# Three first-product blocks kept in SBUF across the end of the gate-table stage

## The chip, the core and the metric

The kernel runs on one core of a Trainium2 chip. The metric is the device time of one execution in microseconds; times of before are the median of three runs and one profiled execution. Engines are named as in the profile: PE is TensorE, PEld its weight load, DVE is VectorE, ACT is ScalarE, POOL is GpSimd, SP is SyncE, whose only work is to issue DMAs.

## The reference, cut to what matters

Two layers, each a token mixer and then an expert channel mixer ("PEER") over 16384 experts. The change touches the channel mixer alone:

```python
def peer(h, wq, keys, u_tab, v_tab):
    q = (t @ wq).reshape(T, PEER_HEADS, 2, PEER_DHALF)
    s = jnp.einsum('thpd,hpkd->thpk', q, keys)
    sv, si = lax.top_k(s, PEER_TOPK)
    ...
    experts = jnp.take_along_axis(cidx, fi, axis=-1)
    gates = jax.nn.softmax(fv, axis=-1)
    ...
        a = jax.nn.gelu(jnp.einsum('tkd,td->tk', u_tab[ec], xc))
        return jnp.einsum('tk,tkd->td', a * gc, v_tab[ec])
```

Each token picks 128 experts (8 heads, 16 each), takes the gelu of its product with their rows of `u_tab`, weights it with the gates, and sums their rows of `v_tab`.

## The kernel before

For most tokens the kernel does not gather: it computes all 16384 experts densely and multiplies by a gate table that is zero where an expert was not picked. The experts come in 128 blocks of 128. For block i, `u_phase(i)` loads a 512 KB weight tile (`u_t`), splits it into two parts (`load_split`: ScalarE makes `whi`, VectorE `wlo`), makes the first product with 24 matmuls (`proj`, L314 to L316) and lets ScalarE take the gelu into an SBUF tile `a` (L824). Such a block is called a projection block. Later `prep` multiplies `a` by the block's gates (L1047, VectorE) and splits the result into `ahi` (L1052, ScalarE) and `alo` (L1053, VectorE), and the second product with rows of `v_tab` follows, again 24 matmuls per 512 KB tile (L1089 to L1091 in layer 0, L1073 in layer 1): a value block.

A layer's channel mixer has three stages:

1. The top-k search (`topk`), on VectorE for the most part.
2. The gate table: for each 16 tokens VectorE makes four one-hot products (`oj`, `oi`, two `wo`; L981 to L986), TensorE multiplies them (L994), ScalarE brings the result to SBUF (`gs`, L996), stores 1 MB to the DRAM table `gd` (L998) and copies the first eight blocks' part to `gt` (L999), which group 0 of the loop uses. There are 32 such steps in layer 0 and 24 in layer 1.
3. The expert loop: 16 groups of 8 blocks. Each group loads its gates (`gt` from `gd`, L1033), preps its 8 blocks and runs its value blocks; in layer 0 the results are added to `x_l` by VectorE (L1092), in layer 1 they stay in PSUM.

While stages 1 and 2 run, TensorE computes projection blocks ahead of the loop: `AHEAD` = 70 of the 128 in layer 0 and 62 in layer 1, spread evenly over the block numbers. Since they do not fit, ScalarE stores each to the DRAM buffer `ad` (L826) and `prep` reads it back (L1043). `upto`, called after each step of the two stages, says how many blocks and how many gather jobs should have been issued by then, from `AHP`, `AHT`, `TKP` and `TKT`. The other 58 (66) blocks are computed in the loop, in `prep`.

For the tokens that are not treated densely (256 in layer 0, 128 in layer 1) GpSimd gathers one row per partition (L835) and VectorE takes a dot (`u_job`, L840) or adds a weighted row (`v_job`, L851): 512 and 256 jobs, each with a 512 KB gather. In the loop `pace` spreads what is left of them over the steps.

The order on each engine is not that of the code: the framework's scheduler sets it when the program is built. Buffers come from pools. A pool that is opened where another was closed takes its bytes, and its first tiles wait for the last users of the old ones. Before, the pools of stage 2 are opened in the order `gsp` (two table tiles `gs` of 8 KB per partition), `mid` (the picks), `spill` (two `a` tiles), then working tiles; after them, at the same place, the loop opens four `ahi`/`alo` pairs (layer 0), `stash` (five `a` tiles), `rx` (three more buffers for `raw` tiles) and six more pairs. `raw` tiles, weights and gathers alike, take turns in a ring of six buffers plus, in the loop, these three.

## Time and profile before

| | us |
|---|---|
| median of 3 runs | 3904.5 (3897.5 to 3907.6) |
| profiled execution | 3904.18 |
| its span, first to last instruction | 3902.4 |
| TensorE busy | 3644.7 (93%), weight loads 3038.8 (78%) |
| VectorE busy | 3208.8 (82%) |
| ScalarE busy | 1493.1 (38%) |
| GpSimd busy | 1064.6 (27%) |

In the profiled execution layer 0's gate table runs from about 973 to 1221 and its expert loop to about 2326; layer 1's gate table ends at about 3063, its loop at 3902. A row of a timeline gives start, duration, engine, line, operation and tiles, and in brackets how long the engine sat idle before it and what ended that. DMA records give the issue, not the landing: when a transfer has landed is read from who waited for it. The engines' busy share is a mean over stages with different limits, so the stages are read apart.

### The profile page before, as it was taken

Reading aid. Unit: us, or ns where it says so; the run is one execution under the profiler, and the core shown is the slowest. Engines: PE = TensorE matmul, PEld = TensorE weight load, DVE = VectorE, ACT = ScalarE, POOL = GpSimd, SP = SyncE. Lnnn points to the kernel's source line nnn. Section 1 sums busy time; section 2 is a strip of 40 time slices with the busy share of each in tenths; the row PEclk is TensorE's granted clock in tenths of the full one; section 3 lists DMA queues with packets and bytes.
Section 4 is the critical chain, followed back from the end, with each engine's and each line's share of the span. In section 5 each row is a group of like instructions: output and inputs, shape, how many; then the busy total and the mean of one; then the engine's idle time right before and its main releaser. Section 6 shows DMA issues by size and latency. Waiting matters only on the chain.

```text
span 3902.4 us, 52533 instructions
## 1 busy us (share of the span) xinstructions
PE 3644.7 (93%) x18725; PEld 3038.8 (78%) x18725; DVE 3208.8 (82%) x6734; ACT 1493.1 (38%) x2115; POOL 1064.6 (27%) x782
## 2 busy tenths in 40 slices
PE   8989889999996999999999989898999999999998
PEld 4777777877775777777777777678999888888887
DVE  7865799998998888888988878548999788788887
ACT  4244433323665222222322233433348533333333
POOL 0000001144332454445555510000000334344441
PEclk9989889999997999999999999899999999999999
DMA  7711134488997999899999947004457999999995
GB/s 249 224 48 45 43 97 157 152 299 289 338 348 277 320 332 313 320 318 335 332 329 323 339 173 251 22 1 141 130 174 285 321 344 341 343 348 337 345 343 187
DMA packets 377663, 967.04 MB, mean 248 GB/s; under 512 B 30632, under 2 KB 160472, under 8 KB 369848
## 3 DMA queue, kind: packets, MB, share of 16 engines
q1 hardware_dynamic: 239048, 468.13, 35.4%
q0 software_dynamic: 111280, 406.28, 29.3%
q10 hardware_dynamic: 27072, 89.27, 5.8%
q8 instruction: 147, 2.41, 0.2%
q14 instruction: 116, 0.95, 0.1%
HBM read 872.20 MB, written 91.36 MB: 247 GB/s over the span
## 4 chain that ended last, share of the span: by engine, by line
PE 41%; issue 10%; DMA 7%; DVE 6%; POOL 5%; ACT 2%; ACTq 0%; POOLq 0%; SPq 0%; DVEq 0%
PE sc L1073 9%; PE mm L314 6%; PE mm L315 6%; PE mm L316 6%; POOL raw L835 5%; PE tp L1073 4%; DMA raw<-in_v_n_dram,E 2%; PE sc L1089 2%; PE sc L1090 2%; PE sc L1091 2%; DVE ht L851 1%; DMA gt<-gd 1%; DVE wlo L163 1%; PE mm L592 1%; DMA raw<-in_u_n_dram,E 1%
## 5 line engine op out<-in xcount | busy, mean ns | idle before, releaser
L162 ACT ACTIVATE whi<-raw 128x1024 fp32r<-128x1024 f32 x640 | 676.5, 1060 | 1501.0 <-PE mm L315 612.3
L835 POOL DMA_INDIRECT raw<-in_u_n_dram,E x384 | 511.2, 1331 | 2226.2 <-DVE wlo L163 1031.4
L314 PE MATMUL mm<-hi_l,whi 128*128 128x512 f32 (+1 forms) x2656 | 995.9, 375 | 11.8 <-ACT whi L162 5.7
L316 PE MATMUL mm<-hi_l,wlo 128*128 128x512 f32 (+1 forms) x2656 | 988.9, 372 | 7.6 <-DVE wlo L163 7.5
L315 PE MATMUL mm<-lo_l,whi 128*128 128x512 f32 (+1 forms) x2656 | 990.7, 373 | 4.5 <-DVE lo_l L294 4.3
L163 DVE TENSOR_TENSOR wlo<-raw,whi 128x1024 fp32r<-128x1024 f32 x640 | 781.2, 1223 | 178.4 <-ACT whi L162 169.9
L835 POOL DMA_INDIRECT raw<-in_v_n_dram,E x384 | 547.7, 1426 | 545.8 <-DVE ht L851 268.6
L314 PEld LDWEIGHTS mm<-hi_l,whi 128*128 128x128 f32 x2656 | 502.7, 189 | 85.5 <-ACT whi L162 6.4
L316 PEld LDWEIGHTS mm<-hi_l,wlo 128*128 128x128 f32 x2656 | 502.2, 189 | 78.0 <-DVE wlo L163 13.5
L315 PEld LDWEIGHTS mm<-lo_l,whi 128*128 128x128 f32 x2656 | 502.9, 189 | 76.9 <-DVE lo_l L294 9.3
L840 DVE SCALAR_TENSOR_TENSOR raw<-raw,ht 128x1024 f32<-128x1024 f32 x384 | 465.9, 1223 | 102.3 <-DMA raw<-in_u_n_dram,E 101.6
L851 DVE SCALAR_TENSOR_TENSOR ht<-raw,wg,ht 128x1024 f32<-128x1024 f32 x381 | 488.6, 1283 | 41.3 <-DMA raw<-in_v_n_dram,E 38.9
L1089 PE MATMUL sc<-ahi,whi 128*128 128x512 f32 x1024 | 399.7, 398 | 34.2 <-DVE x_l L1092 30.5
L1090 PE MATMUL sc<-alo,whi 128*128 128x512 f32 x1024 | 407.4, 399 | 24.4 <-DVE alo L1053 23.6
L1091 PE MATMUL sc<-ahi,wlo 128*128 128x512 f32 x1024 | 404.1, 395 | 0.9 <-DVE wlo L163 0.9
L1052 ACT ACTIVATE ahi<-a 128x512 fp32r<-128x512 f32 (+1 forms) x256 | 147.0, 577 | 394.2 <-DVE a L1047 392.6
L1089 PEld LDWEIGHTS sc<-ahi,whi 128*128 128x128 f32 x1024 | 194.3, 190 | 87.1 <-DVE x_l L1092 23.5
L1090 PEld LDWEIGHTS sc<-alo,whi 128*128 128x128 f32 x1024 | 195.5, 191 | 77.5 <-DVE alo L1053 38.4
L996 ACT ACTIVATE gs<-sc 128x1024 f32<-128x1024 f32 x112 | 214.1, 2021 | 64.0 <-PE sc L994 59.6
L1091 PEld LDWEIGHTS sc<-ahi,wlo 128*128 128x128 f32 x1024 | 195.6, 191 | 41.7 <-DVE wlo L163 1.8
L1047 DVE TENSOR_TENSOR a<-a,gt 128x512 f32<-128x512 f32 (+1 forms) x256 | 158.0, 621 | 64.6 <-DMA gt<-gd 39.7
L1053 DVE TENSOR_TENSOR alo<-a,ahi 128x512 fp32r<-128x512 f32 (+1 forms) x256 | 157.5, 622 | 11.7 <-ACT ahi L1052 11.3
(310 smaller groups left out, 4933.5 us busy)
## 6 DMA issues: line engine op xcount, KB each, us to landing
raw<-in_u_t_dram SPq DMA_DIRECT2D x256, 512.0 KB
raw<-in_v_b_dram SPq DMA_DIRECT2D x128, 512.0 KB
raw<-in_v_n_dram SPq DMA_DIRECT2D x128, 512.0 KB
gd<-gs ACTq DMA_DIRECT2D x56, 1024.0 KB
raw<-in_w_adt_dram SPq DMA_DIRECT2D x64, 512.0 KB
gt<-gd SPq DMA_DIRECT2D x15, 2048.0 KB
raw<-in_wq_dram SPq DMA_DIRECT2D x48, 512.0 KB
gt<-gd SPq DMA_DIRECT2D x15, 1536.0 KB
```

The lines of the kernel that those rows point to most:

```text
L162: nc.scalar.activation(hi, raw, AF.Copy)
L163: nc.vector.tensor_tensor(lo, raw, hi.bitcast(F32), op=ALU.subtract)
L314: nc.tensor.matmul(ps, whi[:, k], hhi[:, k], start=(k == 0), stop=False)
L315: nc.tensor.matmul(ps, whi[:, k], hlo[:, k], start=False, stop=False)
L316: nc.tensor.matmul(ps, wlo[:, k], hhi[:, k], start=False, stop=(k == K - 1))
L835: nc.gpsimd.indirect_dma_start(out=g, out_offset=None, in_=tab, in_offset=bass.IndirectOffsetOnAxis(ap=G["E"][:, it, k:k + 1], axis=0), el ...
L840: nc.vector.scalar_tensor_tensor(g, g, 1.0, G["ht", it], op0=ALU.mult, op1=ALU.mult, accum_out=G["dots", it][:, k:k + 1])
L851: nc.vector.scalar_tensor_tensor(G["acc", it], g, G["wg", it][:, k:k + 1], G["acc", it], op0=ALU.mult, op1=ALU.add)
L1073: nc.tensor.matmul(accs[t][h], w[:, sl], v[:, halves[h]], start=(i == 0 and j == 0), stop=(i == NKEYS - 1 and j == 2))
L1089: nc.tensor.matmul(ps, vh[:, c], wh, start=(c == 0), stop=False)
L1090: nc.tensor.matmul(ps, vh[:, c], wl, start=False, stop=False)
L1091: nc.tensor.matmul(ps, vl[:, c], wh, start=False, stop=(c == GS - 1))
```

## The change

Three more blocks per layer are computed ahead, at the end of the gate-table stage: the first three block numbers that are not spilled (0, 2 and 4 in layer 0; 0, 1 and 3 in layer 1). They are not stored; `upto` keeps the tile in `kept`, and `prep` takes it from there. `AHT` grows by three, so that the schedule of blocks ends at 73 and 65. In the loop these blocks no longer call `u_phase` nor `pace`, and the number of steps over which jobs are spread is smaller by six. For the tiles to survive, the pool `stash` is opened before the gate-table stage, at the other end of SBUF, and serves that stage's spilled blocks too; `spill` lives only in the top-k stage; and `gsp` is opened within the gate-table stage, behind `mid`.

```diff
-AHT = [50, 38]
+AHT = [53, 41]
...
+CARRY = 3
...
             spilled = sorted(order)
+            carry = [i for i in range(NKEYS) if i not in order][:CARRY]
+            early = spilled + carry
+            kept = {}
...
             def upto(nu, nt):
-                while nxt[0] < min(nu, AHEAD[l]):
-                    u_phase(spilled[nxt[0]])
+                while nxt[0] < min(nu, len(early)):
+                    kept[early[nxt[0]]] = u_phase(early[nxt[0]])
                     nxt[0] += 1
                 tick(nt - done[0])
...
             with ExitStack() as es1:
-                gsp = es1.enter_context(tc.tile_pool(name=nm("gsp"), bufs=2))
                 mid = es1.enter_context(tc.tile_pool(name=nm("mid"), bufs=1))
-                cur["st"] = es1.enter_context(tc.tile_pool(name=nm("spill"), bufs=SPB))
...
                 with ExitStack() as es2:
+                    cur["st"] = es2.enter_context(tc.tile_pool(name=nm("spill"), bufs=SPB))
                     tp_ = es2.enter_context(tc.tile_pool(name=nm("topk"), bufs=1))
...
+                cur["st"] = es.enter_context(tc.tile_pool(name=nm("stash"), bufs=STB, side="right"))
                 with ExitStack() as es2:
+                    gsp = es2.enter_context(tc.tile_pool(name=nm("gsp"), bufs=2))
                     tw = es2.enter_context(tc.tile_pool(name=nm("gw"), bufs=2))
...
             with ExitStack() as es2:
                 vps = [] if last else [es2.enter_context(tc.tile_pool(name=nm("vp"), bufs=4))]
-                cur["st"] = es2.enter_context(tc.tile_pool(name=nm("stash"), bufs=STB))
...
-                nstep = (NKEYS - AHEAD[l]) * PWU[l] + NKEYS - PEND[l]
+                nstep = (NKEYS - AHEAD[l] - CARRY) * PWU[l] + NKEYS - PEND[l]
...
                         nc.sync.dma_start(A, ad[order[i], :, :TD])
+                    elif i in carry:
+                        A = kept.pop(i)
                     else:
                         A = u_phase(i)
...
-                    if i not in order:
+                    if i not in order and i not in carry:
                         pace(PWU[l])
```

What the scheduler made of it is seen in the order of instructions. The program up to the end of layer 0's top-k search is the same. In all three places below a row is line, operation, output tile and input tiles; line numbers of the changed kernel are one to six higher.

ScalarE, end of layer 0's gate table and the first preps of group 0. `gs` and `gt` are the last table tile and its copy, `whi` splits of weights, `a` a gelu. Before:

```order
L998 DMA gd<-gs_11470 128x2048
L999 ACTIVATE gt_5781<-gs_11470 128x128
L1052 ACTIVATE ahi_11670<-a_11667 128x512
L1052 ACTIVATE ahi_11686<-a_11683 128x512
L162 ACTIVATE whi_11746<-raw_11744 128x1024
L162 ACTIVATE whi_11803<-raw_11801 128x1024
L1052 ACTIVATE ahi_11724<-a_11721 128x512
L1052 ACTIVATE ahi_11740<-a_11737 128x512
L843 ACTIVATE wg_121<-dots_120 128x128
L162 ACTIVATE whi_11857<-raw_11855 128x1024
L162 ACTIVATE whi_11895<-raw_11893 128x1024
L824 ACTIVATE a_11775<-mm_11750 128x512
```

And now:

```order
L1003 DMA gd<-gs_11576 128x2048
L1004 ACTIVATE gt_5781<-gs_11576 128x128
L1058 ACTIVATE ahi_11736<-a_11646 128x512
L1058 ACTIVATE ahi_11743<-a_11740 128x512
L1058 ACTIVATE ahi_11748<-a_11679 128x512
L1058 ACTIVATE ahi_11755<-a_11752 128x512
L1058 ACTIVATE ahi_11760<-a_11712 128x512
L828 ACTIVATE a_11802<-mm_11777 128x512
L163 ACTIVATE whi_11865<-raw_11863 128x1024
L163 ACTIVATE whi_11900<-raw_11898 128x1024
L1058 ACTIVATE ahi_11805<-a_11802 128x512
```

Before, two of the four unspilled blocks of group 0 still had their weights split (`whi_11746`, `whi_11803`) and their first product made behind the table; now `a_11646`, `a_11679` and `a_11712` are there, and the splits that come next are of value weights.

SP's queue at the same place: `raw` are weight tiles, `a` spilled blocks that are read back. Before:

```order
L159 DMA raw_12119<-in_u_t_dram 128x1024
L159 DMA raw_11744<-in_u_t_dram 128x1024
L159 DMA raw_11855<-in_v_b_dram 128x1024
L159 DMA raw_11968<-in_v_b_dram 128x1024
L1043 DMA a_11794<-ad 128x512
L159 DMA raw_12079<-in_v_b_dram 128x1024
L1043 DMA a_11848<-ad 128x512
L159 DMA raw_12166<-in_v_b_dram 128x1024
L1033 DMA gt_12117<-gd 128x32x128
```

And now:

```order
L160 DMA raw_12136<-in_v_b_dram 128x1024
L160 DMA raw_11863<-in_v_b_dram 128x1024
L1047 DMA a_11764<-ad 128x512
L1047 DMA a_11818<-ad 128x512
L160 DMA raw_11974<-in_v_b_dram 128x1024
L1037 DMA gt_12085<-gd 128x32x128
```

The first load into one of the three extra buffers was `raw_11744`, the weights of a projection block, and waited for the last table matmul; it is now `raw_11863`, the weights of the second value block, and waits for ScalarE and for DMAs out of the table tiles too.

TensorE, end of layer 1's gate table: L905 and L912 make rows for the final step, `mm` of L314 to L316 (L315 to L317) are projection blocks, L1073 (L1079) is the first value block. Before:

```order
L316 MATMUL mm_27256<-hi_l_22374,wlo_27253 128x384
L905 MATMUL mm_27305<-c_ident,mods 128x128 x4
L905 MATMUL mm_27311<-c_ident,mods 128x128 x4
L912 MATMUL mm_27317<-c_ident,x_l 128x128 x4
L912 MATMUL mm_27323<-c_ident,x_l 128x128 x4
...
L912 MATMUL mm_27359<-c_ident,x_l 128x128 x4
L314 MATMUL mm_27377<-hi_l_22374,whi_27373 128x384
```

And now:

```order
L317 MATMUL mm_27360<-hi_l_22374,wlo_27357 128x384
L909 MATMUL mm_27404<-c_ident,mods 128x128 x4
L1079 MATMUL sc_27466<-whi_27491,ahi_27471 128x512 x2
L1079 MATMUL sc_27466<-wlo_27492,ahi_27471 128x512 x2
L1079 MATMUL sc_27467<-whi_27491,ahi_27471 128x512 x2
```

The first value block now follows the last kept block and one group of L905; the other nine groups of L905 and L912 stand between the first value blocks.

## Rows read from the trace of the kernel before

**Rows 1.** Windows of 20 us, layer 0; columns in the first row.

```profile
core 0: us, PE busy (x) PEld busy (x) DVE busy (x) ACT busy (x) POOL busy (x), PEclk, DMA share, GB/s
1160.00:1180.00 20.00, 12.48 (x111) 10.65 (x110) 19.97 (x22) 11.62 (x11) 5.04 (x3) 0.83 0.97 356
1180.00:1200.00 20.00, 10.23 (x98) 9.17 (x98) 18.93 (x21) 13.79 (x11) 3.36 (x2) 0.64 0.66 247
1200.00:1220.00 20.00, 11.80 (x126) 10.84 (x125) 12.82 (x11) 15.22 (x11) 1.09 (x2) 0.76 0.52 213
1220.00:1240.00 20.00, 15.02 (x54) 11.41 (x55) 15.34 (x23) 7.54 (x12) 8.15 (x6) 0.75 0.83 293
1240.00:1260.00 20.00, 13.13 (x48) 9.39 (x47) 15.31 (x25) 5.97 (x8) 8.76 (x7) 0.91 0.78 267
1260.00:1280.00 20.00, 20.00 (x90) 16.57 (x89) 16.76 (x24) 3.19 (x3) 10.68 (x8) 1.00 1.00 364
```

**Rows 2.** Timeline of layer 0's joint: start, us, engine, line, tiles [idle, releaser].

```profile
1210.56 2.36 DVE L986 TENSOR_TENSOR wo<-oi,wh 128x2048 f16<-128x2048 f16 x2
1221.11 2.50 DVE L1047 TENSOR_TENSOR a<-a,gt 128x512 f32<-128x512 f32 x4 [8.19 <-ACT gt L999]
...
1220.39 0.33 ACTq L998 DMA_DIRECT2D gd<-gs  x1
...
1222.97 1.99 ACT L162 ACTIVATE whi<-raw 128x1024 fp32r<-128x1024 f32 x2
...
1256.19 2.01 ACT L162 ACTIVATE whi<-raw 128x1024 fp32r<-128x1024 f32 x2 [2.99 <-PE sc L1090]
...
1196.55 22.14 SPq L159 DMA_DIRECT2D raw<-in_u_t_dram  x2
...
1224.07 0.79 PE L314 MATMUL mm<-hi_l,whi 128*128 128x512 f32 x1 [5.73 <-ACT whi L162]
```

**Rows 3.** VectorE by line, 977 to 1213: count, busy, mean ns, idle before.

```profile
L840 DVE SCALAR_TENSOR_TENSOR raw<-raw,ht 128x1024 f32<-128x1024 f32 x49 | 59.9, 1223 | 11.9 <-DMA raw<-in_u_n_dram,E 11.8
...
L163 DVE TENSOR_TENSOR wlo<-raw,whi 128x1024 fp32r<-128x1024 f32 x24 | 29.3, 1222 | 0.0
L840 DVE DVE_READ_ACCUMULATOR raw<-raw,ht 128x1 f32 x49 | 4.2, 85 | 0.0
```

**Rows 4.** Windows of 20 us at layer 1's joint.

```profile
3060.00:3080.00 20.00, 19.29 (x123) 17.93 (x122) 8.25 (x11) 11.36 (x17) 6.93 (x5) 1.00 1.03 379
3080.00:3100.00 20.00, 15.25 (x65) 13.22 (x65) 13.01 (x19) 5.75 (x8) 5.61 (x4) 0.83 0.94 335
```

**Rows 5.** Timeline of layer 1's joint, then one wait of SP there.

```profile
3067.51 1.95 PE L905 MATMUL mm<-c_ident,mods 128*128 128x128 f32 x16
...
3074.69 0.45 PE L314 MATMUL mm<-hi_l,whi 128*128 128x384 f32 x1
...
3088.03 2.08 PE L1073 MATMUL sc<-whi,ahi 128*128 128x512 f32 x4 [4.75 <-ACT whi L162]
...
3063.13 0.33 ACTq L998 DMA_DIRECT2D gd<-gs  x1
...
3072.74 0.38 SPq L1033 DMA_DIRECT2D gt<-gd  x1
...
SPq L1033 <- DMA gd<-gs: 0.2, 1, 0.2
```

**Rows 6.** Windows of 100 us in the two expert loops.

```profile
1460.00:1560.00 100.00, 91.49 (x388) 73.44 (x389) 81.42 (x122) 25.65 (x32) 45.15 (x36) 0.98 0.91 316
...
3360.00:3460.00 100.00, 100.00 (x486) 88.16 (x485) 80.00 (x120) 37.48 (x50) 40.26 (x32) 1.00 0.95 342
```

**Rows 7.** Waits in layer 0's loop, 1260 to 2290: us, times, longest.

```profile
PE sc L1089 <- DVE x_l L1092: 28.4, 20, 4.6
PE sc L1090 <- DVE alo L1053: 18.8, 16, 4.2
...
DVE ht L851 <- DMA raw<-in_v_n_dram,E: 38.3, 23, 4.4
```

## The prediction

> **What bounds the kernel now.** I read the page's 40 slices first, to find the stages, and then the two places where a layer passes from its gate table to its expert loop. A projection block is 24 matmuls (L314 to L316), a value block 24 (L1089 to L1091, or L1073 in layer 1).
>
> The loops are bound by TensorE, the second one plainly: from 3360 to 3460 it is busy 100.00 of 100 us at full clock, while in layer 0's loop 91 of 100 us are busy [rows 6]. What is missing there are waits at the joints of the 16 groups: 28.4 us for the x_l update and 18.8 us for alo, both on VectorE [rows 7]. So a microsecond of TensorE work that leaves a loop for a place where TensorE stood idle should come back whole in layer 1 and nearly whole in layer 0.
>
> Such a place is the end of layer 0's gate table. VectorE runs there without a pause and TensorE is busy only 12.48, 10.23 and 11.80 of each 20 us between 1160 and 1220, with the clock falling to 0.64 [rows 1]. In this whole table stage VectorE's only wait of weight is 11.9 us, for gathers [rows 3]: the stage lasts as long as VectorE's list. Then follows a joint. VectorE starts its last pair of gate products at 1210.56, ScalarE issues the last table store at 1220.39, VectorE starts the first a x gt product at 1221.11, and TensorE starts at 1224.07 on two projection blocks, since the weights of the first were asked for at 1218.69 (1196.55 + 22.14, the load that stood in SP's queue until its buffer came free) and split at 1222.97 [rows 2]. The first pair of value blocks ends only at 1256.19, where ScalarE's wait on L1090 ends [rows 2], and the clock is down again in between: 15.02 and 13.13 busy of 20 us [rows 1].
>
> Layer 1's joint is smaller. Its table stage is bound by TensorE; TensorE then goes through the 10 groups of L905 and L912 (3067.51 to 3074.69) and two blocks, waits 4.75 us, and starts the first value block at 3088.03 [rows 5], in a stretch whose clock is 0.83 [rows 4].
>
> **The change, part by part.** Nothing is computed less. 132 blocks are still spilled and read back; the three kept ones never were spilled. So all of it is order.
>
> Layer 0, end of the table stage. By the order, 74 projection blocks instead of 72 stand ahead of the last table matmul: all four unspilled blocks of group 0 (before, two of them stood behind it). VectorE has three splits more before its last gate product and six gather dots fewer, since the kept blocks no longer pace dots. 3 x 1.22 = 3.7 less 6 x (1.22 + 0.09) = 7.9 gives 4.2 us less busy time; starts lie some 0.08 us closer than durations, so 4 us [rows 3]. The extra matmuls cost nothing: two blocks are 2 x 24 x 0.22 = 10.7 us (90 matmuls in the 20 us from 1260 [rows 1]) against 25 us of idle TensorE. ScalarE's three splits of 1 us lie in its waits for TensorE. The first a x gt product moves from 1221.1 to 1217.1.
>
> The joint itself. The first value block needs no late load and can begin at about 1218.5, as fast as VectorE and ScalarE make ahi and alo. The second cannot: its load raw_11863 goes into one of the three extra raw buffers, which by the new pool order lie over the table's staging buffers, so SP holds it until the last table store has landed. Behind it in SP's queue stand both spilled activations of group 0 and a further weight load; ScalarE's split of it stands ahead of the last three ahi, so TensorE waits. The price: the store is issued 0.7 us before the product, at 1216.4. The trace does not show when layer 0's last store lands. Nearest below: a 512 KB load takes at most 1222.97 - 1218.69 = 4.3 us [rows 2]. Above: layer 1's last store, issued at 3063.13, holds gt<-gd back until 3072.74, 9.6 us, with the DMA at 1.03 [rows 4, 5], against 0.52 here [rows 1]. I take 7, in the middle: 1223.4. Then 0.4 to issue and 4.3 to load (1228.1), 1.1 for the split on ScalarE, and 33 matmuls of the pair that are still to run: 14 at the lower of the clock's two levels, 1.2 GHz, at 0.44 each (6.2 us; the stretch from 1220 shows 0.75 of full speed in the same place [rows 1]) and 19 at 0.22 (4.2). The pair ends at 1239.6, between 1237 and 1242 by the two ends of the store. Before, it ended at 1256.2; as many blocks (54 projections, 126 value blocks) are left at either point. **Gain 16.6 us** (14 to 19).
>
> What layer 0's loop has to take back: six dots on VectorE and their six gathers. If all of it lay on the path, 6 x 1.31 = 7.9 us; hidden, nothing. VectorE is busy 81 of 100 us there [rows 6], nearer to hidden: I take **2.5 us lost**. The groups behind the first keep their pattern of splits, dots and updates, in slightly other places; for that I allow 8 us either way, a sixth of the 47 us of [rows 7].
>
> Here a rule speaks against the change. The row first: from 1460 to 1560 matmuls are busy 91.49 and weight loads 73.44 of 100 us, VectorE 81.42, the DMA engines 0.91 [rows 6]. The Trainium skill (Perfetto Trace Analysis, Identifying the Most-Contended Engine) says that matmul busy time is no good measure of how close TensorE is to its limit, that the share of weight loads is, and that the most contended engine is the one to relieve. By that, TensorE would not be the bound in layer 0's loop, and blocks moved out of it would give nothing lasting: that is the first rival. Layer 1's rows, at 100 for matmuls and 88.16 for weight loads, fit either reading.
>
> Layer 1. Two blocks more stand ahead of the last table matmul, and three behind it in place of four; one g2 group, instead of all 10 groups of L905 and L912, comes before the first value block. TensorE is the bound here, so the last table matmul comes 2 x 4.0 us later (a block is 384 wide, three quarters of 5.3), and the last store is issued at 3071.1, landing at 3080.7 by the 9.6 us above; alo of the first value block takes bytes under that store. TensorE's own list has one block more (4.0) and 6.3 us fewer of L905 and L912: 3088.0 - 4.75 + 4.0 - 6.3 = 3081.0, just behind the store. VectorE has four dots instead of eight ahead of the first product, so fewer gathers to wait for. The idle 4.75 us go, and of the 3.4 us that the clock lost in 3080 to 3100 [rows 4] I count 2.5, as part of that stretch was idle: **gain 7 us**. Nothing here is bounded from below by a mechanism; if the store lands later than 3081, TensorE waits for it, and at 7 us later the gain is gone: 0 to 9.
>
> **Sum.** 16.6 - 2.5 + 7 = 21 us. The profiled execution took 3904.2 us (span 3902.4), the median is 3904.5, so no correction: 3904 - 21 = **3883 us**. Its own range, all bounds together: 14 - 7.9 + 0 - 8 to 19 + 9 + 8, 3904 less 36 and plus 2, that is 3868 to 3906, most of it 3872 to 3893.
>
> **Rivals.**
> 1. The gain is given back in layer 0's loop. For it: DMA engines busy 0.91 and 316 GB/s there [rows 6], and the order puts 12 dots more into groups 2 to 16, so 12 gathers of 512 KB: 6.3 MB, 19.9 us at 316 GB/s. Against it: at the next joint the DMA still had a tenth free, and TensorE's waits name VectorE. Time: 3904 - 24 + 20 = 3900, no change that can be told.
> 2. The joint of layer 0 stays long: the new wait takes the place of the old. If the store takes 9.6 us and the load behind it another 9.6, as it shares the engines with gathers and the spilled activations, the pair ends at 1248: gain 8 there, 12.5 in all, 3892. For it: the new wait stands on SP with two loads behind it. Against it: DMA at 0.52 in the stretch.
> 3. Slower: the joints of layer 0's groups grow. In VectorE's list each x_l update stands behind dots that wait for gathers; TensorE waits 3.1 us per joint now (47.2 over 15). One gather wait more in front of an update costs 1.7 us on average (38.3 over 23) and at worst 4.4 [rows 7]. At 2.2 us more per joint the 21 us and the 11.7 us of the bound below are used up (33 over 15): slower begins there. With 2.8 us: 3904 - 21 + 42 = 3925. Against it: the pattern of updates and dots per group is nearly the same in both orders.
> 4. The change does not do what it says: the order moves the three blocks, but in the table stage only two more stand ahead of layer 0's last table matmul, and if VectorE there is not the bound, the table ends 10.7 us later and takes the gain with it: 3904 - 16.6 + 10.7 - 7 + 2.5, or 3894. [Rows 1] speak against it.
>
> **How the numbers follow.** The measurement of this kernel can tell about 0.3%, 11.7 us, so faster means below 3892.8 and slower above 3916.2. Forecast (3883): 0.64, of which 0.58 lies below 3892.8 and 0.06 above it. Rival 1: 0.14, within. Rival 2: 0.08, of which 0.05 faster, 0.03 within. Rival 3: 0.07, slower. Rival 4: 0.07, of which 0.02 faster, 0.05 within. Faster: 0.58 + 0.05 + 0.02 = 0.65. Within: 0.06 + 0.14 + 0.03 + 0.05 = 0.28. Slower: 0.07. Range: from 3868, both gains and the reorder at their upper bounds, to 3903, which takes in rivals 2 and 4 and most of rival 1; beyond it lie rival 3 and the tail of rival 1.
>
> **What would show it.** In the changed kernel's 20 us windows TensorE should be busier between 1160 and 1200; the last table copy should come at 1214 to 1219, the first pair of value blocks should end by 1242, with a wait for whi of the second block just before; layer 1's first value block should start near 3088 less the earlier gain (about 3067) with no idle of several us before it, and layer 0's loop should last as long from there as it did. I am wrong if layer 0's table ends later than 1222, if SP's held load lands after 1235, if waits for x_l and alo in groups 2 to 16 add up to much over 47 us, or if layer 1's first value block waits for the store.

## The result, and the profile after

The changed kernel takes 3882.0 us (median of 20 runs), the kernel before 3907.8 in the same session: ratio 0.994, 95% interval 0.9927 to 0.9954. The forecast was 3883. One of the 20 runs took 5071.9 us at a granted clock of 0.654, where the others show 0.96; the ratio leaves it out. The sum came out, but largely by luck: of its four terms only one has the right sign, and a gain of 6 us was not among them. That is seen when the two kernels are cut into stretches. There are two profiles of each (the second ones are the first two experiments); all times are in us from the trace. The forecast's 12.6 is for the end of the first pair of value blocks; its row goes by the first x_l update, which follows 2 to 6 us later:

| stretch | before | forecast | after |
|---|---|---|---|
| start to layer 0's last table copy (L999) | 1221.1, 1225.3 | -4 | 1228.2, 1220.1 |
| from there to the first x_l update | 37.0, 36.9 | -12.6 | 23.5, 20.6 |
| layer 0's loop, first to last x_l update | 1064.9, 1064.3 | +2.5 | 1060.1, 1057.7 |
| from there to layer 1's first table matmul | 587.0, 586.0 | 0 | 580.9, 580.7 |
| from there to the end of layer 1's value blocks | 974.4, 978.1 | -7 | 981.5, 981.5 |
| rest | 18.0, 18.0 | 0 | 18.0, 18.0 |
| span | 3902.4, 3908.6 | -21 | 3892.2, 3878.6 |

By the means: +1, -15, -6, -6 and +5, together -20. The medians differ by 25.8 us; the two profiles of each don't place the rest.

Layer 0's joint, first profile after, in the windows of [rows 1] (same columns):

```profile
1160.00:1180.00 20.00, 20.00 (x136) 16.40 (x136) 16.92 (x19) 13.98 (x14) 6.89 (x5) 1.00 0.91 336
1180.00:1200.00 20.00, 15.42 (x132) 12.52 (x130) 18.98 (x22) 10.91 (x10) 5.05 (x4) 0.96 0.93 326
1200.00:1220.00 20.00, 10.47 (x98) 9.53 (x97) 19.19 (x18) 12.40 (x10) 0.00 (x0) 0.59 0.61 246
1220.00:1240.00 20.00, 12.39 (x58) 9.65 (x58) 10.71 (x15) 12.83 (x16) 5.65 (x3) 0.69 0.55 197
1240.00:1260.00 20.00, 13.25 (x48) 9.84 (x47) 10.98 (x18) 2.76 (x4) 7.57 (x7) 0.83 0.97 324
1260.00:1280.00 20.00, 20.00 (x90) 16.55 (x89) 19.10 (x29) 4.43 (x5) 14.75 (x11) 1.00 0.80 282
```

TensorE is fuller from 1160 to 1200, with the kept blocks, as forecast. Its clock still falls behind that, to 0.59 between 1200 and 1220, where it is busy 10.47 of 20 us and waits for gate products. The same joint in the timeline (start, us, engine, line, tiles, in brackets idle and releaser), to be held against [rows 2]:

```profile
1227.51 0.33 ACTq L1003 DMA_DIRECT2D gd<-gs  x1
...
1228.95 3.04 ACT L1058 ACTIVATE ahi<-a 128x512 fp32r<-128x512 f32 x5 [0.76 <-DVE a L1053]
...
1235.31 2.01 ACT L163 ACTIVATE whi<-raw 128x1024 fp32r<-128x1024 f32 x2 [2.15 <-DMA raw<-in_v_b_dram]
...
1245.75 2.00 ACT L163 ACTIVATE whi<-raw 128x1024 fp32r<-128x1024 f32 x2 [3.67 <-PE sc L1096]
...
1204.13 27.68 SPq L160 DMA_DIRECT2D raw<-in_v_b_dram  x2
```

The last store goes out at 1227.51, 7 us later than before. SP is through with the load that it held for it at 1231.8, ScalarE waits only 2.15 us for its data, and the first pair of value blocks ends at 1245.75: 17.5 us behind the table's end, where it was 35.1. Behind the pair TensorE then waits for the x_l update (waits of TensorE from 1100 to 1262: us, times, longest):

```profile
PE sc L1095 <- DVE x_l L1098: 6.1, 1, 6.1
```

The update stands in VectorE's list behind a dot that waits 4.24 us for its gather. That is why the table above shows less of the gain for this profile; in the second one the wait is 3.51 us.

Layer 1's joint, in the windows and lines that answer to [rows 4, 5], SP's, ScalarE's and VectorE's rows and one of TensorE's:

```profile
3060.00:3080.00 20.00, 15.61 (x75) 13.13 (x73) 8.22 (x12) 2.86 (x5) 5.87 (x5) 0.91 0.79 271
3080.00:3100.00 20.00, 13.72 (x61) 11.18 (x61) 13.16 (x21) 8.13 (x14) 6.32 (x5) 0.74 0.77 272
```

```profile
3066.99 0.38 SPq L1037 DMA_DIRECT2D gt<-gd  x1
3067.42 8.91 SPq L160 DMA_DIRECT2D raw<-in_u_t_dram  x1
...
3052.03 0.31 ACT L1004 ACTIVATE gt<-gs 128x128 f32<-128x128 f32 x1 [0.40 <-ACT gs L1001]
...
3083.63 1.06 ACT L163 ACTIVATE whi<-raw 128x1024 fp32r<-128x1024 f32 x1 [12.66 <-DMA raw<-in_u_t_dram]
...
3047.13 1.23 DVE L844 SCALAR_TENSOR_TENSOR raw<-raw,ht 128x1024 f32<-128x1024 f32 x1 [6.56 <-DMA raw<-in_u_n_dram,E]
...
3056.73 1.22 DVE L844 SCALAR_TENSOR_TENSOR raw<-raw,ht 128x1024 f32<-128x1024 f32 x1 [7.23 <-DMA raw<-in_u_n_dram,E]
...
3064.16 1.23 DVE L844 SCALAR_TENSOR_TENSOR raw<-raw,ht 128x1024 f32<-128x1024 f32 x1 [5.05 <-DMA raw<-in_u_n_dram,E]
...
3066.45 0.55 DVE L1053 TENSOR_TENSOR a<-a,gt 128x384 f32<-128x384 f32 x1
...
3085.23 3.04 PE L916 MATMUL mm<-c_ident,x_l 128*128 128x128 f32 x12 [6.17 <-ACT g2row L911]
```

The table is ready at 3052.3, but VectorE's first product comes 14 us later, behind dots that wait 5 to 7 us each. Then ScalarE waits 12.66 us for a load that SP needed 8.91 us to issue, right behind gt<-gd. TensorE starts the first value block at 3067.6, as forecast, and then runs dry: 29.3 of 40 us busy in these windows, 34.5 in those before. Its longest wait, 6.17 us, is for a copy of ScalarE's (`g2row`) that stands behind the split of that late load.

### The profile page after: what moved, and what is told of

It is laid out like the page before. It is cut to its first block, busy times and chain, and to the rows that moved or that the text cites. A ratio compares the mean times of both kernels' runs of the same rounds, so it can differ in the third digit from the quotient of the medians.

```text
span 3892.2 us, 52526 instructions
## 1 busy us (share of the span) xinstructions
PE 3644.0 (94%) x18725; PEld 3040.4 (78%) x18725; DVE 3207.2 (82%) x6734; ACT 1489.3 (38%) x2115; POOL 1070.7 (28%) x782
## 4 chain that ended last, share of the span: by engine, by line
PE 54%; issue 14%; DMA 11%; DVE 10%; POOL 6%; ACT 4%; ACTq 0%; POOLq 0%; SPq 0%; DVEq 0%
PE sc L1079 9%; PE mm L315 9%; PE mm L316 9%; PE mm L317 9%; POOL raw L839 6%; PE tp L1079 4%; DMA raw<-in_u_n_dram,E 3%; DMA raw<-in_v_n_dram,E 3%; PE mm L593 2%; DVE wlo L164 2%; PE sc L1095 1%; PE sc L1096 1%; PE sc L1097 1%; PE tp L590 1%; DVE xr L220 1%
## 5 line engine op out<-in xcount | busy, mean ns | idle before, releaser
L839 POOL DMA_INDIRECT raw<-in_u_n_dram,E x384 | 519.6, 1353 | 2242.5 <-DMA raw<-in_v_n_dram 793.4
L315 PE MATMUL mm<-hi_l,whi 128*128 128x512 f32 (+1 forms) x2656 | 993.6, 374 | 7.1 <-ACT a L828 3.8
L317 PE MATMUL mm<-hi_l,wlo 128*128 128x512 f32 (+1 forms) x2656 | 987.4, 372 | 11.8 <-DVE wlo L164 11.8
L316 PE MATMUL mm<-lo_l,whi 128*128 128x512 f32 (+1 forms) x2656 | 989.1, 372 | 3.8 <-DVE lo_l L295 3.6
L164 DVE TENSOR_TENSOR wlo<-raw,whi 128x1024 fp32r<-128x1024 f32 x640 | 779.9, 1220 | 174.0 <-ACT whi L163 163.8
L317 PEld LDWEIGHTS mm<-hi_l,wlo 128*128 128x128 f32 x2656 | 501.3, 189 | 81.5 <-DVE wlo L164 16.3
L315 PEld LDWEIGHTS mm<-hi_l,whi 128*128 128x128 f32 x2656 | 501.8, 189 | 78.2 <-ACT a L828 4.7
L316 PEld LDWEIGHTS mm<-lo_l,whi 128*128 128x128 f32 x2656 | 501.5, 189 | 75.6 <-DVE lo_l L295 8.3
L844 DVE SCALAR_TENSOR_TENSOR raw<-raw,ht 128x1024 f32<-128x1024 f32 x384 | 464.6, 1220 | 103.3 <-DMA raw<-in_u_n_dram,E 102.6
```

What stands on the lines that cost most here:

```text
L164: nc.vector.tensor_tensor(lo, raw, hi.bitcast(F32), op=ALU.subtract)
L315: nc.tensor.matmul(ps, whi[:, k], hhi[:, k], start=(k == 0), stop=False)
L316: nc.tensor.matmul(ps, whi[:, k], hlo[:, k], start=False, stop=False)
L317: nc.tensor.matmul(ps, wlo[:, k], hhi[:, k], start=False, stop=(k == K - 1))
L839: nc.gpsimd.indirect_dma_start(out=g, out_offset=None, in_=tab, in_offset=bass.IndirectOffsetOnAxis(ap=G["E"][:, it, k:k + 1], axis=0), el ...
L844: nc.vector.scalar_tensor_tensor(g, g, 1.0, G["ht", it], op0=ALU.mult, op1=ALU.mult, accum_out=G["dots", it][:, k:k + 1])
```

## Experiments

A stage is named by the table above. A profile is one execution; the ratios are against runs of the kernel before on the same chip.

**Two more profiles.** No edit.

> The kernel before, unchanged, for a second profiled execution. Theory (the 7 us by which layer 0's table stage ended later in the changed kernel's profile, and the 6 us by which its layer 1 mixers were shorter, are scatter between executions): the two executions of one kernel differ by several us at the same milestones. Last table copy of layer 0 between 1218 and 1230 us, table end to end of the first pair of value blocks 33 to 38 us. Rival (the stages repeat to within 1 us, and the order makes the difference): last table copy at 1220 to 1222, layer 1's first table matmul as far behind layer 0's last x_l update as in the first profile (587 us).

Layer 0's last table copy came at 1225.3 (before: 1221.1), the four stretches behind it were within 4 us of the first profile, three of them within 1. So the theory holds for the table's end, the rival for the stretch ahead of layer 1's table: its 6 us are not scatter.

> The changed kernel, unchanged, for a second profiled execution. Theory: 0.994 of the time before; table end of layer 0 to end of the first value pair again 16 to 20 us (35.1 in the kernel before), in layer 1 again a wait of ScalarE of 10 to 14 us for a u_t load that SP issues right behind gt<-gd, so that layer 1's value blocks start about 20 us and end about 10 us earlier than before. The last table copy of layer 0 anywhere between 1215 and 1230. Rival (the layer 1 wait was an accident of that execution): the wait is under 5 us and the value blocks' start and end gain the same.

Ratio 0.9947 (0.9926 to 0.9967). The last table copy came at 1220.1, 8 us earlier than in the first profile; the first pair ended 17.2 us behind it (theory: 16 to 20), joint 20.6 us, layer 1 again 981.5, with a wait of ScalarE of 12.7 us for the u_t load. So the start up to the table's end scatters by some 8 us from execution to execution. The other stretches of these two kernels repeat within 4 us, the two last ones of the changed kernel within 0.2: layer 1's loss is a property of the order. (In a kernel profiled twice below, layer 0's loop differs by 9 us, so a single profile doesn't settle a few us there.)

**The pools without the blocks.**

```diff
-AHT = [53, 41]
+AHT = [50, 38]
...
-CARRY = 3
+CARRY = [0, 0]
...
```

Where `CARRY` is used, `CARRY[l]` now stands, so that the lists hold layer 0's and layer 1's number.

> The pools of the change without any kept block (same counts of blocks, splits and dots in each stage as before). Theory 1 (the gain is the order of the blocks at the two joints): no difference, ratio 0.998 to 1.002, table end to first value pair 33 to 38 us. Rival 2 (the pools' new places free buffers earlier and bring the gain by themselves): ratio 0.994, the joint of layer 0 at 17 to 23 us.

0.9978 (0.9962 to 0.9994), just below theory 1's range and clear of 1: neither theory as it stands. Layer 0's joint stayed at 38.1 us, so the joint is the blocks' doing. But layer 0's loop took 1059.9 and the stretch up to layer 1's first table matmul 581.9: the pools alone bring some 5 us in each of two stretches that the prediction gave them nothing for. (The run with kept blocks in layer 1 alone, further down, repeats both: 1061.5 and 581.6.) Two waits of the second stretch, from 2370 to 2405, before and with the pools:

```profile
ACT cb L215 <- DMA cb<-in_cb_dram: 6.0, 1, 6.0
...
DVE xr L219 <- ACT cb L215: 2.8, 1, 2.8
```

```profile
ACT cb L216 <- DMA cb<-in_cb_dram: 3.2, 1, 3.2
...
DVE xr L220 <- ACT cb L216: 1.0, 1, 1.0
```

A load of layer 1's first mixer is waited for 3 us less. But in the same window ScalarE waits longer for its other weights (21.5 us against 15.4), so what makes the 5 us is not shown.

**Is it the far end of SBUF?** The kernel before, with one argument more:

```diff
-                cur["st"] = es2.enter_context(tc.tile_pool(name=nm("stash"), bufs=STB))
+                cur["st"] = es2.enter_context(tc.tile_pool(name=nm("stash"), bufs=STB, side="right"))
```

> The kernel before with one word more: the activation pool of the expert loop stands at the other end of SBUF, opened where it was; no kept block and the other pools as before. It tells what the pool's place alone does of the 8.6 us by which the new pools without kept blocks were faster (layer 0's loop 1060 us against 1064.6, layer 1 from layer 0's last update to its first table matmul 582 us against 586.5). Theory 1 (what counts is which old buffers the next stage's first loads lie over, so the far end gives it all): ratio 0.997 to 0.999, both stretches at 1060 and 582. Rival 2 (it is the order of the pools in the table stage): ratio 0.9995 to 1.001, both stretches as before.

1.0018 (1.0001 to 1.0036), loop 1068.9, the later stretch 586.4: both stretches are no shorter than before, as in rival 2, and the time is a little above its range. The pool's end alone brings nothing; by exclusion it takes the other moves too (the pool opened ahead of the table stage and serving it, and the new order there). Which of these moves does it, and by which buffer, was not separated.

**Each layer alone.**

```diff
-AHT = [53, 41]
+AHT = [53, 38]
...
-CARRY = 3
+CARRY = [3, 0]
...
```

> The change in layer 0 alone: three kept blocks and the new pools there, layer 1 with no kept block and 38 blocks in its table stage as before. Theory 1 (layer 0's joint brings most of it, less what the table stage loses): ratio 0.9955 to 0.9975, 10 to 17 us; layer 0's last x_l update 10 to 15 us earlier than before, layer 1's table end to the end of its value blocks as long as before. Rival 2 (layer 0's loop gives the gain back and layer 1 brings the whole): ratio 0.999 to 1.001. Rival 3 (layer 0 alone brings everything and layer 1's part is void): ratio 0.9935 to 0.995.

> The kernel with the change in layer 0 alone, once more, against the kernel before: in its first run it was 0.9905 of the time before, which is 28 us under the new pools without kept blocks, while the stages in its profile account for some 21. Theory 1 (the stages are what it is: joint of layer 0 16 us shorter, loop 5 to 8, layer 1's first half 6, layer 1's joint and value blocks as before): ratio 0.990 to 0.993; table end to first x_l update 20 to 22 us, layer 0's loop 1055 to 1060, last update to layer 1's first table matmul 579 to 582, from there to the end of the value blocks 973 to 976. Rival 2 (its first run was lucky and the kept blocks of layer 1 cost nothing): ratio 0.994 or above, as the changed kernel.

First 0.9905 (0.9883 to 0.9927), better than any of its three theories allowed, then 0.9934 (0.992 to 0.9948), between its two. In the two profiles: joint 20.8 and 24.4, loop 1057.0 and 1048.1, layer 1's first half 579.9 and 580.4, its second 974.5 twice. So layer 0's half brings everything, and layer 1's half takes 7 us back in the profiles. In time the two versions' intervals touch, so that leaving out layer 1's half is faster still is likely but not shown.

```diff
-AHT = [53, 41]
+AHT = [50, 41]
...
-CARRY = 3
+CARRY = [0, 3]
...
```

> The change in layer 1 alone: new pools, three kept blocks in layer 1, layer 0 without a kept block. Theory 1 (pools bring 8 to 12 us in both layers, the kept blocks of layer 1 cost 5 to 8): ratio 0.998 to 1.001; layer 1 from first table matmul to the end of its value blocks 980 to 983 us against 974 to 978; layer 0's table end to its first x_l update 36 to 39 us as before. Rival 2 (the prediction's step: the kept blocks of layer 1 gain 7 us): ratio 0.995 to 0.997, that stage 966 to 971 us.

1.0007 (0.999 to 1.0023), layer 1's second half 982.2, layer 0's joint 37.8. Theory 1: against the pools alone (0.9978; 975.0) the kept blocks of layer 1 cost 7 us in the profile and some 11 in time, though the two intervals just overlap. The prediction's step for layer 1 falls.

**What holds layer 1's joint: the load behind gt<-gd?** The edit swaps the two in SP's queue.

```diff
-                    if last and c == 1:
+                    if last and c == (6 if g == 0 else 1):
                         load_gt(g + 1)
```

> The changed kernel with one swap in SP's queue at layer 1's joint: the u_t load that stood right behind gt<-gd (1.5 MB in rows of 512 bytes) now stands ahead of it; every other row of the order is the same. In the changed kernel's two profiles the issue of that load takes 8.9 us and ScalarE then waits 12.7 us for its data. Theory 1 (SP cannot issue the next transfer until it has worked off the many small rows of gt<-gd, and that is what layer 1 loses): the load's issue takes under 1 us, ScalarE's wait for it goes or falls under 4 us, layer 1 from its first table matmul to the end of its value blocks takes 973 to 977 us in place of 981.5, ratio to the kernel before 0.992 to 0.993. Rival 2 (the wait only moves to the a<-ad loads that now stand behind gt<-gd): the stage stays at 980 to 982, ratio 0.9945. Rival 3 (the 8.9 us are a wait for the last table store to land, whatever stands ahead): the load's issue stays at about 8.9 us.

0.9926 (0.991 to 0.9942), stage 979.6. SP's queue in this kernel, and two of the waits from 3037 to 3105:

```profile
3060.01 0.80 SPq L160 DMA_DIRECT2D raw<-in_u_t_dram  x2
3060.87 0.43 SPq L1037 DMA_DIRECT2D gt<-gd  x1
3061.36 11.40 SPq L1047 DMA_DIRECT2D a<-ad  x2
```

```profile
ACT ahi L1058 <- DVE a L1053: 16.1, 4, 9.1
...
DVE raw L844 <- DMA raw<-in_u_n_dram,E: 22.8, 4, 7.4
```

Now the loads pass in 0.80 us for two and the blocks that are read back stand for 11.40: the long issue belongs to whatever follows gt<-gd, so rival 3 (a wait for the store) falls and theory 1's mechanism stands. Its price does not: ScalarE's wait for the load is gone, but the stage is only 2 us shorter. VectorE's waits for gathers are still there, and it waits 4.4 us for a<-ad. By the stage rival 2 is nearer; the ratio lies in theory 1's range, but its interval takes in rival 2's too.

**The loads behind gt<-gd, a v_n and a u_t load, moved ahead with the change in layer 0 alone** (`c == (4 if g == 0 else 1)`):

> The change in layer 0 alone, as in the run with that, and in layer 1 (without kept block) gt<-gd put behind the two loads that stood right behind it in SP's queue, a v_n and a u_t load; TensorE's order is the same. Theory 1 (the 7 us that an issue behind gt<-gd takes also delay layer 1's first value blocks of the kernel before): table end to first value block of layer 1 18 to 23 us in place of 26.6, ratio 0.988 to 0.9895. Rival 2 (that joint waits for something else, such as VectorE's list or the store): 25 to 28 us, ratio as in the run with layer 0 alone, 0.9905.

0.9908 (0.9888 to 0.9927); table end to first value block 23.7 us, between the two ranges, but the stage 973.4 against 974.5: rival 2.

**Or the dots?** Layer 1's gather jobs start ten paces later.

```diff
+DLY = [0, 10]
...
-                    tick(max(0, min(rest, int(rest * step[0] / nstep)) - (rest - (len(jobs) - done[0]))))
+                    dl = DLY[l]
+                    tick(max(0, min(rest, int(rest * (step[0] - dl) / (nstep - dl))) - (rest - (len(jobs) - done[0]))))
```

> The changed kernel with layer 1's gather dots starting ten paces later in its loop (none is left out). In the changed kernel's two profiles VectorE does five of these dots ahead of its first a x gt product of layer 1, each waiting 5 to 7 us for a gather that was issued only when the dot before it had freed its buffer; the first product starts 13 to 14 us after the last table copy although the table is ready. Theory 1 (this chain of gather, dot, gather holds the joint of layer 1): without the five dots the first product starts within 3 us of the last table copy, layer 1 from its first table matmul to the end of its value blocks takes 966 to 973 us in place of 981.5, ratio to the kernel before 0.990 to 0.992. Rival 2 (the u_t load behind gt<-gd holds it, whatever VectorE does): first product early, but the stage stays at 978 to 982, ratio 0.994. Rival 3 (the dots come back later in the loop, whose gathers are then denser): joint shorter, value blocks longer by the same, ratio 0.994.

1.0009 (0.999 to 1.0027). The table ends at 3040.5; VectorE's first product in the timeline, and windows of 20 and then 100 us (of the five dots that the expectation counts, four stand ahead of the product and one behind it):

```profile
3043.05 0.55 DVE L1055 TENSOR_TENSOR a<-a,gt 128x384 f32<-128x384 f32 x1
```

```profile
3040.50:3060.50 20.00, 20.00 (x115) 18.34 (x113) 8.48 (x11) 8.13 (x13) 3.03 (x3) 1.00 0.96 335
3060.50:3080.50 20.00, 17.68 (x84) 14.76 (x83) 11.84 (x18) 9.11 (x14) 6.91 (x5) 0.91 0.63 204
...
3100.00:3200.00 100.00, 92.25 (x425) 79.83 (x424) 65.94 (x98) 30.13 (x41) 35.03 (x28) 0.96 0.83 275
3200.00:3300.00 100.00, 96.86 (x466) 84.47 (x465) 77.56 (x116) 33.28 (x46) 42.50 (x32) 1.00 0.94 328
```

Theory 1 is right about the joint: product 2.5 us behind the table, TensorE busy 37.7 of the 40 us behind the table, where the changed kernel's two profiles show 27.4 and 26.1 and the kernel before 34.6 and 31.3. But the loop then pays more than that back, as rival 3 said and beyond it: TensorE misses 8 and 3 us per 100 where the changed kernel has 100.00, VectorE waits 38.2 us for gathers from 3100 to 3300 where that one waits 12.1, and the stage takes 1003.1. Why the delayed gathers come so much less in advance of their dots was not tested.

The same delay with the change in layer 0 alone:

> The change in layer 0 alone with the same delay of layer 1's dots by ten paces. VectorE of the kernel before does eight dots ahead of its first a x gt product of layer 1, which starts 20.9 us after the last table copy. Theory 1 (the chain of gathers holds this joint too, kept blocks or not): the stage from the first table matmul to the end of the value blocks takes 966 to 971 us in place of 974.5, ratio 0.988 to 0.989. Rival 2 (without kept blocks ahead the joint needs its late loads, which end no sooner): 973 to 975 us, ratio 0.9905. Against the run with the kept blocks in both layers and the same delay it tells whether the kept blocks of layer 1 are worth anything once the dots are out of the way: by theory 1 of that run they are level or 2 to 4 us better.

0.9989 (0.9972 to 1.0006): the stage takes 1001.3, the same loss in the loop, and the joint is hardly shorter (25.1 us from table to first value block). But here the delay did not clear VectorE's list: three dots still stand ahead of the first product, with waits of 3.0, 6.8 and 0.4 us, and the product comes 20.5 us behind the table. So with kept blocks the dots and their gathers hold this joint; what holds it without them this run doesn't tell.

**Layer 0's held load.** Twelve loads go to the old buffers before the three extra ones are used in layer 0.

```diff
-        pool = cur["rx"] if cur.get("rx") and ring[0] % (RAWB + RXB) >= RAWB else cur["raw"]
+        pool = cur["rx"] if cur.get("rx") and ring[0] >= 0 and ring[0] % (RAWB + RXB) >= RAWB else cur["raw"]
...
-                    ring[0] = -1
+                    ring[0] = -1 if last else -7
```

> The changed kernel with layer 0's first twelve weight loads behind its gate table in the six buffers of the old pool, so that the load of the second value block (raw_11863 in the changed kernel) no longer lies over the table's staging buffers and doesn't wait for the last table store. Theory 1 (the held load costs the joint little, since the store lands 4.4 us after its issue and ScalarE waits 2 us for the load): table end to first x_l update 18 to 21 us against 20.4 to 23.5. Rival 2 (the held load sets the joint, as the prediction had it, with its 10 us from the first product to the end of the load): 13 to 17 us.

Joint 21.7 us, just above theory 1's range and as in the changed kernel: the load that waits for the last store does not set it. In its place VectorE's waits for gathers (2.98 and 2.38 us) stand ahead of alo, and the blocks read back from DRAM are asked for only at 1238.3, 8 us behind the table. One run took 3926.5 us, the loss lying in layer 0's loop (1088.7, where 1048 to 1060 is seen otherwise): the turn in which loads and gathers share the ring of buffers seems worth some 28 us there, by one execution.

## Why the forecast came out, step by step

**The end of layer 0's table: wrong.** "Three splits more, six dots fewer, 4 us earlier" is the step that failed. The stage from the first one-hot product to the last gate product, VectorE's splits and dots, before and after ([rows 3] cut at another place; after the bar busy and mean, then idle before):

```profile
L840 DVE SCALAR_TENSOR_TENSOR raw<-raw,ht 128x1024 f32<-128x1024 f32 x53 | 64.7, 1223 | 15.8 <-DMA raw<-in_u_n_dram,E 15.7
...
L163 DVE TENSOR_TENSOR wlo<-raw,whi 128x1024 fp32r<-128x1024 f32 x26 | 31.8, 1222 | 0.0
```

```profile
L844 DVE SCALAR_TENSOR_TENSOR raw<-raw,ht 128x1024 f32<-128x1024 f32 x50 | 60.9, 1221 | 18.4 <-DMA raw<-in_u_n_dram,E 18.4
...
L164 DVE TENSOR_TENSOR wlo<-raw,whi 128x1024 fp32r<-128x1024 f32 x31 | 37.8, 1219 | 0.0
```

Five splits more and three dots fewer lie in it (four and two by their starts, since the windows cut one of each). The other four dots were dropped ahead of the stage, where it gained nothing: the first table matmul comes at 966 us on average with and without kept blocks. And fewer dots did not wait less. The stage takes 258.0 us, before 250.7 (260.5 and 253.3 in the second profiles). From the first table matmul to the last table copy it is 257.3 to 264.3 us in the nine profiles with kept blocks in layer 0 and 251.5 to 255.3 in the five without: some 5 us longer, not 4 shorter. Rival 4 had the table late by 10.7 us, with VectorE not the bound. That holds from 1160 to 1180 alone, where TensorE is busy 20.00 us and VectorE 16.92; over the stage VectorE is busy 239.4 of 258.0.

**The joint: right, and better than its terms.** From the table's end the pair was forecast to end after 22.5 us in place of 35.1; it took 17.5 (17.2 in the second profile). Over all profiles the first x_l update follows the table's end by 36.9 to 39.4 us without kept blocks and by 19.4 to 24.4 with them. The mis-sized term is the store: 7 us to land (4.3 to 9.6) was taken, but SP had the held load out 4.3 us after the store's issue, the lower bound; the load's data were there 7 us behind the first product, not 11. Rival 2 falls, and the experiment on that load shows that it isn't the limit any more. Not in the working was the wait behind the pair, 6.1 us in the first profile for an x_l update behind a dot: rival 3's mechanism, at this one joint.

**Layer 0's loop: wrong sign.** 2.5 us were to be lost, 6 were gained. The waits of [rows 7], in the first profile after and nearly the same window (1255 to 2280):

```profile
PE sc L1095 <- DVE x_l L1098: 21.7, 19, 4.5
PE sc L1096 <- DVE alo L1059: 17.7, 17, 3.1
```

39.4 us in place of 47.2. These two are not all: waits for ScalarE's ahi grew from 1.8 us to 6.0. With every wait of TensorE from the first to the last x_l update counted, it is 53.7 and 51.2 us in the two profiles before and 51.5 and 43.9 in the two after. They did not grow, nor did the loop, so rivals 1 and 3 fall. Most of the 6 us are the pools': without kept blocks in layer 0 they reach 1059.9 and 1061.5, with them it is 1048 to 1060 (but for the run on the held load). So the six dots that the loop took back cost nothing that can be told.

For rival 1 the prediction had named a rule of the Trainium skill (Perfetto Trace Analysis, Identifying the Most-Contended Engine): the share of weight loads tells how near TensorE is to its limit. By the 73 of 100 us TensorE would not be the bound in this loop. But a window of [rows 1] shows what that share is worth here: from 1260 to 1280 matmuls are busy 20.00 of 20 us at full clock and weight loads 16.57, or 83 of 100. Held against that, 73 is almost nine tenths of a full TensorE. And the 15 us gained at the joint were not given back.

**Between the layers: not in the sum.** 6 us, of which the pools alone bring 5. The prediction asked which buffers the first tiles behind the gate table lie over, and did not ask it of layer 1's first stage. That the answer there is such a buffer is not shown.

**Layer 1: wrong sign.** The forecast was 7 us gained, the profiles show 5 to 7 lost. The table term was near (159.6 us against 153.8 from first table matmul to last copy; +8.0 forecast). The first value block came where it was forecast, at 3067.6, but by luck: the stages ahead had gained more than forecast. From layer 1's first table matmul it was 174.9 us, where the forecast makes 171 and the first profile before shows 178. The loss is idle time of TensorE; the windows are the whole stretch, before and after (columns as in [rows 1]):

```profile
2910.00:3884.40 974.40, 967.69 (x5329) 865.08 (x5328) 797.25 (x969) 432.42 (x528) 332.32 (x256) 1.00 0.90 322
```

```profile
2892.70:3874.20 981.50, 968.90 (x5329) 866.45 (x5328) 795.33 (x969) 430.96 (x528) 333.66 (x256) 0.99 0.89 320
```

It is busy as long, and idle 12.6 us in place of 6.7 (13.9 and 10.1 in the second profiles). Two steps failed. "VectorE has four dots instead of eight ahead of the first product, so fewer gathers to wait for": behind the last one-hot product it has four instead of seven, but the four wait 21 us for their gathers (in both profiles), the seven waited 15.5 (19 in the second). They now run one at a time, each gather issued when the dot before it has freed a buffer. Three dots of the first profile before, 4 to 5 us apart, then GpSimd's rows of the first profile after, with the wait before each; the dots shown above are 7 to 10 us apart:

```profile
3069.76 1.23 DVE L840 SCALAR_TENSOR_TENSOR raw<-raw,ht 128x1024 f32<-128x1024 f32 x1 [4.25 <-DMA raw<-in_u_n_dram,E]
...
3074.36 1.23 DVE L840 SCALAR_TENSOR_TENSOR raw<-raw,ht 128x1024 f32<-128x1024 f32 x1 [2.23 <-DMA raw<-in_u_n_dram,E]
...
3078.36 1.23 DVE L840 SCALAR_TENSOR_TENSOR raw<-raw,ht 128x1024 f32<-128x1024 f32 x1 [2.76 <-DMA raw<-in_u_n_dram,E]
```

```profile
3039.71 1.68 POOL L839 DMA_INDIRECT raw<-in_u_n_dram,E  x1 [6.50 <-DVE raw L844]
3048.64 1.68 POOL L839 DMA_INDIRECT raw<-in_u_n_dram,E  x1 [7.25 <-DVE raw L844]
3058.24 1.68 POOL L839 DMA_INDIRECT raw<-in_u_n_dram,E  x1 [7.92 <-DVE raw L844]
3065.66 1.68 POOL L839 DMA_INDIRECT raw<-in_u_n_dram,E  x1 [5.75 <-DVE raw L844]
```

And "the idle 4.75 us go": 3.45 us stayed ahead of the first value block, and 6.17 came behind it. The projection blocks that filled this joint before are the kept ones, made while TensorE was full anyway (159.6 of 159.6 us busy), so behind the table it has little to do while VectorE's gathers and the load behind gt<-gd come round. In layer 0 the blocks moved into idle time of TensorE; in layer 1 they moved into full time and left idle time behind. "Nothing here is bounded from below by a mechanism" was the warning in the text; the bound (0) should have been below zero.

So the joint of layer 0 was right, and it is the one term of the four that was. That the sum was met is luck: the 10 us that the pools bring, in no term, and what the joint and the loop did better than forecast made up for the table's end (5 us) and for layer 1 (12 us, from 7 gained to 5 lost). Of the signs that the prediction named, the table's end missed 1214 to 1219 (1220.1, and 1228.2, beyond the 1222 at which it called itself wrong), and the pair's end missed "by 1242" in the first profile (1245.75).

## What to carry to other kernels

Work moved ahead of a joint helps where the engine that does it stood idle ahead of the joint, and hurts where it was full there and idle behind; look at both sides of each joint before crediting it. Count dropped work by the stage in which it lies, and waits by what feeds them: four dots waited longer here than seven. When pools move, ask of every stage that opens buffers afterwards, and test the pools alone.

## What the runs showed of the hardware

An issue on SP behind gt<-gd (1.5 MB in rows of 512 bytes in layer 1) stands long: 8.91, 8.87, 8.68 and 9.10 us in four profiles with kept blocks in layer 1 where a load follows at once, 6.66 in the first profile before, 5.89 with the later dots, and 11.40 for two a<-ad. A load that SP reached 4.7 us later stood the rest (second profile after):

```profile
3103.94 0.38 SPq L1037 DMA_DIRECT2D gt<-gd  x1
3108.67 4.20 SPq L160 DMA_DIRECT2D raw<-in_v_n_dram  x1
```

It ends 8.9 us behind the start of gt<-gd, while gt<-gd itself shows 0.38 us and most other issues 0.33 to 0.43. In the first profile after there are 15 such places in layer 1, and in each the next issue ends 6.3 to 9.9 us behind the start of gt<-gd. The Trainium skill (Perfetto Trace Analysis, DMA Instruction — HWDGE (DVE, Sync)) says that a reported issue holds its wait for the unit that makes descriptors, which one transfer locks until all of its descriptors are made, and that the issuing engine is free for its next instruction only then. The rows agree in that a wait shows within the follower's reported time. They differ in that the transfer with the many rows, which by the page would be long itself, is short; why the follower waits is not shown beyond that. In layer 1's full loop it costs nothing, as TensorE stays busy throughout; at the joint it was 12.7 us of ScalarE's time, though only 2 us of the stage's.
